# A hybrid decoder trunk: where the product with VO of the last chunk and M and VO of the first heads stand in the order of work

## The chip, the core and the metric

The program runs on one core of one Trainium2 chip. The metric is device time in microseconds (us) of one execution, lower is better. The core has TensorE (PE, matmuls), VectorE (DVE), ScalarE (ACT), GpSimd (POOL) and SyncE (SP), each with a queue of its own, and DMA engines; they meet only at semaphores.

## The reference

One layer, 2048 prompt tokens and 8 samples, width 1024, all in fp32. The part that the change touches:

```
h = rmsnorm(x, g_cross); q = (h @ wq_c) in 4 heads of 256
s = q @ mem_k.T / 16 ; a = softmax(s) ; o = a @ mem_v          # mem_k = mem @ wk_c, mem_v = mem @ wv_c, 256 memory tokens
x = x + o @ wo_c
h = rmsnorm(x, g_ffn); up = h @ w_up ; c = causal depthwise conv of width 3 (up)
x = x + (silu(c_gate) * c_act) @ w_down
```

Ahead of it stand an input projection of rmsnorm(x) @ w_in to pooling channels, q, k and v, a pooling mixer, a differential attention and an output projection; behind it a last rmsnorm.

## The kernel before, in words

**Tiles.** The prompt is cut into four chunks of 512 tokens (c = 0 to 3; the samples ride with chunk 3). Activations lie transposed, 128 channels on the partitions. Each fp32 operand is split in two: `hi`, a cast on ACT, and `lo`, the rest, a subtraction on DVE (`split`, L94 and L95; for weights `whi` L307 and `wlo` L310, for half weights `whl` L327 and L329). A product is three matmuls (L99 to L101): hi by lo, hi by hi, lo by hi.

**Memory side.** For each head two matrices are made once. M = wq_c(head) mem_k.T (`m_head`: 16 transposes `wqT` L540, then 48 matmuls of 256 columns) gives the scores from h in one product; VO = mem_v wo_c(head) (`vo_head`, 24 matmuls of 512 columns) gives the output from the softmax in one. Both go to DRAM and come back as weights later. `p0_items((0, 1))` makes those of heads 0 and 1 at the start of the program; its list is cut into `kv0`, `m0`, `kv1`, `m1`: keys and values of head 0, M and VO of head 0, and the same for head 1. `half` is the list of input projections `z` (L483) of chunks 0 and 1, with the pooling products `pool` among them; `n1[c]` the norm of chunk c that they need.

**Cross-attention of a chunk** (`p3_items`): `sc_` has per head the scores S in PSUM (96 matmuls of 256 columns), then the softmax: maximum on DVE (`mx`, L1274), `nbx`, four exponentials on ACT (E, L1280), reciprocal and scaling on DVE (L1281, L1282). E is transposed by PE (AT, L1302) and split into Ahi and Alo; the transposes are put off by a delay counted in cost, and forced when the next part needs them. `vo` begins with a reload of x, then has 8 tiles of 24 matmuls of 512 columns, each followed by an add to x on DVE (L1327), and a store. S takes one of two large PSUM buffers, which the up products take too.

**Feed-forward** (`ffn_items`): 22 pairs of an activation tile and a gate tile, in groups of 4, 4, 4, 4, 4 and 2. A pair is seven products of 12 matmuls of 256 columns (L1613, L1615), an algorithm with fewer multiplications, whose sums of inputs (`xop_items`: `t`, `x` L1573, and their splits `xhi`, `xlo`) and of weights (`sums_items`: stored as `s_d`, loaded as `shl`) are made beforehand; the adds of its results are DVE's `s` and `Uf` (L1618). The `down` products (L1729) of a group run among the pairs of the next. `n3` is the norm ahead of it (h3sq L228, scales L271).

**What sets the order.** All work of the program is one list of items, put together by hand at the end of the kernel, and run from front to back by `drive`; every engine takes its instructions in the order in which they are then issued. An item has a cost `i[2]` and a latency `i[3]`. `weave(main, extra, lo, hi)` spreads the list `extra` over the list `main`: from the share lo of main's cost to the share hi. `look(a, b, c)` sets how many weights ahead of their use the load (SP), the cast (ACT) and the subtraction (DVE) are issued.

Of the kernel before, what the change touches and what calls it, by code (L numbers as in the profile page):

```python
# [48 lines left out]
def tile_trunk_step(ctx: ExitStack, tc: tile.TileContext, a, o):  # L49
# [306 lines left out]
    def item(specs, fn, cost=0.0, lat=0.0):  # L356


        return (specs, fn, cost, max(lat, cost, 0.3))
# [17 lines left out]
    def weave(main, extra, lo=0.0, hi=1.0):  # L377

        tm, te = sum(i[2] for i in main) or 1.0, sum(i[3] for i in extra) or 1.0
        out, k, dm, de = [], 0, 0.0, 0.0  # L380
        for i in main:
            out.append(i)
            dm += i[2]
            while k < len(extra) and lo + (hi - lo) * (de / te) <= dm / tm:
                out.append(extra[k])
                de += extra[k][3]
                k += 1
        return out + extra[k:]
# [978 lines left out]
    def both(key, name, src, write):  # L1367

        def fn(n):
            def run(ws):  # L1370
                ps = PB("sx")
                for kt in range(KT):
                    for z in range(2):
                        PE.matmul(ps[:2 * NS, :256], src[:, kt].rearrange("p z b -> p (z b)"), ws[kt // 4][z][:, kt % 4, :],
                                  start=kt == 0 and z == 0, stop=kt == KT - 1 and z == 1)
                if n == 0:
                    sx[key] = H("sx")
                S.copy(sx[key][:2 * NS, n * 256:(n + 1) * 256], ps[:2 * NS, :256])
                if n == 3:
                    later(2.0, write)  # L1380
            return run
        return [item([cols256(name, n * 256, 0), cols256(name, n * 256, 1)], fn(n), 2.0) for n in range(4)]
# [110 lines left out]
    sc_items = both("q", "wq_c", h2st, sc_qwrite) + [item([], lambda _: None, 0, 5.0)]  # L1493
# [272 lines left out]
    def tail_half(t):  # L1766
        def fn(_):
            ps, m = tail_turn(t, 0)
            V.tensor_tensor(tail["y"][t][:m, :512], ps[:m, :512], tail["g"][:m, :512], ALU.mult)
        return item([], fn, 0.5)  # L1770
# [69 lines left out]
                         t[:FT, :512].rearrange("n (b p) -> n b p", b=4))  # L1840


    def ffn_items(c, xops):


        out, dn, j = [], dn0.pop() if dn0 else [], 0
        for g in GROUPS:
            if j == GROUPS[0]:
                out.append(item([], ffn_open(c)))
            last = j + g == NF  # L1850
            for i in range(g):
                u = ffn_up(c, j + i)
                k = (2, 1)[i] if last else (2, 3, 3, 0)[i]
                d, dn = dn[:k], dn[k:]
                at = (5, 6, 7) if i == 0 else (2, 4, 6)
                for k, up in enumerate(u):
                    out.append(up)
                    if last and i == g - 1:
                        out += xops[k - 1:k] if k else []
                    if k + 1 in at:  # L1860
                        out += d[:1]
                        d = d[1:]
            if last:
                out += xops[6:]
            out += dn
            dn = ffn_down(c, j, g)
            j += g
        if c == NCH - 1:
            return out + [item([], conv_out)] + dn[:5] + [tail_half(t) for t in range(3)] + dn[5:7] + [
                tail_half(t) for t in range(3, 5)] + dn[7:] + [item([], tail_out)]  # L1870
        dn0.append(dn)
        return out

    dn0 = []
    n1 = [norm1_items(c) for c in range(NCH)]
# [3 lines left out]
    def raw_open(_):  # L1879
# [5 lines left out]
    half = p1_items((0, 1))  # L1885
    pre = p0_items((0, 1))
    att01, att23 = att_items((0, 1)), att_items((2, 3))
    kv0, m0, kv1, m1 = pre[1:13], pre[13:23], pre[23:35], pre[35:]
    order = pre[:1] + [item([], vec_load), look(4, 3, 2)] + kv0[:6] + n1[0][0] + kv0[6:] + [item([], vec_turn)]
    order += weave(weave(kv1, m0), n1[0][1][:3] + n1[1][0] + n1[0][1][3:], 0.1, 1.0)  # L1890
    order += weave(weave(half[:12], m1), [item([], pool_load), item([], lambda_)] + n1[1][1], 0.2, 1.0)
    order += [look(3, 2, 1)]
    order += weave(weave(half[12:24] + [item([], pool_prep)] + half[24:-8], sums_items(range(5)), 0.0, 0.6),
                   n1[2][0] + n1[2][1] + n1[3][0] + n1[3][1][:5] + [item([], att_table)], 0.65, 1.0)
    order += att01[0] + weave(half[-8:], n1[3][1][5:])
    late = p1_items((2, 3))
# [3 lines left out]
    wo, n2, sc_, vo, n3 = zip(*p3)  # L1900
# [3 lines left out]
    order += weave(vo[0], n2[1], 0.0, 0.9)  # L1904
    order += weave(sc_[1] + wo[2], sample_items, 0.0, 0.95)
    order += weave(vo[1] + sc_[2][:8], merge(n2[2], sample_items2[:-2]) + sample_items2[-2:], 0.0, 0.55)
    order += weave(sc_[2][8:] + wo[3] + weave(vo[2], n2[3], 0.0, 0.9) + weave(sc_[3] + vo[3], n3[0] + xop_items(0), 0.4, 1.0),
                   sums_items(range(16, NF)), 0.0, 0.85)
    xops = [xop_items(c) for c in range(1, NCH)] + [[]]
    order += [look(6, 3, 2)]  # L1910
    order += weave(ffn_items(0, xops[0]), sc_items + n3[1], 0.02, 0.9)
    order += weave(ffn_items(1, xops[1]), final(0) + sc_items2 + n3[2], 0.2, 0.9)
    order += weave(ffn_items(2, xops[2]), final(1) + n3[3], 0.2, 0.9)
    order += weave(ffn_items(3, xops[3]), final(2), 0.2, 0.5)
# [30 lines left out]
```

## Time and profile before

| | |
|---|---|
| median of 3 runs | 3116.74 us (3115.84 to 3120.43) |
| the profiled execution | 3116.27 us, its span 3114.6 us |
| mean granted clock of PE | 0.978 |
| PE, DVE, ACT, POOL busy | 94%, 72%, 43%, 17% |

The times of the rows are in us from the start of the span. A hole in front of an instruction is given in brackets with what ended it. In the program, the input projections of the first two chunks begin at 67 us; the scores of the last chunk end at about 1558 us, its product with VO runs until 1615 us, and the first group of four pairs until about 1690 us.

### The profile page before, as it was taken

How to read it: one execution, taken by the hardware profiler on the slowest of the kernel's cores; microseconds unless marked ns; L12 is line 12 of the kernel's file. 1: busy time of each engine (PE TensorE's matmuls, PEld its weight loads, DVE VectorE, ACT ScalarE, POOL GpSimd, SP SyncE). 2: the span in 40 equal slices, each digit the busy share in tenths (PEclk: the TensorE clock that was granted, in tenths of full speed). 3: DMA queues.
4: the chain of work that ended last, by engine and by line, in shares of the span. 5: the costliest groups of instructions: out<-in, count | busy, mean ns of one | idle time of the engine just before them, and what ended most of it. 6: DMA issues, size and time to landing. Idle time of an engine off the chain costs nothing.

```text
span 3114.6 us, 52466 instructions
## 1 busy us (share of the span) xinstructions
PE 2939.9 (94%) x19806; PEld 2650.3 (85%) x19806; DVE 2240.0 (72%) x4032; ACT 1351.9 (43%) x2271; POOL 516.2 (17%) x961
## 2 busy tenths in 40 slices
PE   7999899889899898999989999999999999999998
PEld 6778789778788687689978899888899989999998
DVE  5734666467776668666778978888888777877777
ACT  5534445355665442334333344444444433443333
POOL 0244235312111115421000000010000010000000
PEclk9999999989999999999999999999999999999999
DMA  8777478835353357658759876687776786576762
GB/s 280 243 270 241 135 238 263 265 97 186 115 173 119 110 176 255 203 171 282 276 190 332 294 247 220 211 275 249 238 253 217 236 291 209 178 262 218 240 210 105
DMA packets 520511, 683.14 MB, mean 219 GB/s; under 512 B 27472, under 2 KB 342359, under 8 KB 520243
## 3 DMA queue, kind: packets, MB, share of 16 engines
q1 hardware_dynamic: 466525, 533.87, 52.8%
q0 software_dynamic: 39936, 135.17, 12.2%
q10 hardware_dynamic: 13798, 10.76, 1.1%
q8 instruction: 156, 2.56, 0.3%
q14 instruction: 96, 0.79, 0.1%
HBM read 549.12 MB, written 130.98 MB: 218 GB/s over the span
## 4 chain that ended last, share of the span: by engine, by line
PE 59%; DVE 8%; issue 4%; DMA 2%; ACT 2%; POOL 1%; DVEq 0%; ACTq 0%; POOLq 0%; SPq 0%
PE up L1613 15%; PE down L1729 15%; PE up L1615 7%; PE wo L483 3%; PE upB L1613 2%; PE S L99 2%; PE S L101 2%; PE S L100 2%; PE O L1163 2%; PE vo L99 1%; PE vo L100 1%; PE vo L101 1%; PE upB L1615 1%; PE sc L1111 1%; DVE T L1122 1%
## 5 line engine op out<-in xcount | busy, mean ns | idle before, releaser
L1729 PE MATMUL down<-act,whi 128*128 128x512 f32 (+1 forms) x1760 | 452.1, 351 | 3.2 <-ACT whi L307 3.1
L1613 PE MATMUL up<-xhi,shl 128*128 128x256 f32 (+1 forms) x2816 | 406.9, 285 | 7.9 <-DVE s L1618 6.3
L1613 PEld LDWEIGHTS up<-xhi,shl 128*128 128x128 f32 x2816 | 365.1, 188 | 37.9 <-DVE s L1618 13.2
L1667 ACT ACTIVATE cc<-Uf,vec 128x512 f32<-128x512 f32 (+1 forms) x176 | 143.9, 818 | 502.6 <-DVE Uf L1618 491.6
L310 DVE TENSOR_TENSOR wlo<-wraw,whi 128x1024 fp32r<-128x1024 f32 x256 | 310.2, 1220 | 38.5 <-ACT whi L307 30.2
L1729 PEld LDWEIGHTS down<-act,whi 128*128 128x128 f32 x1760 | 286.5, 189 | 36.6 <-ACT whi L307 3.5
L307 ACT CAST whi<-wraw 128x1024 fp32r<-128x1024 f32 x256 | 265.3, 1047 | 102.3 <-DMA wraw<-in_w_down_dram 29.3
L1729 PE MATMUL down<-act,wlo 128*128 128x512 f32 (+1 forms) x880 | 280.2, 350 | 0.1
L1672 POOL COPY halo<-Uf 128x2 f32<-128x2 f32 x176 | 56.7, 322 | 1275.5 <-DVE Uf L1618 1250.5
L1129 ACT ACTIVATE T<-T,mn 128x1024 f32<-128x1024 f32 (+4 forms) x192 | 171.9, 897 | 131.2 <-DVE mn L1122 120.5
L1615 PE MATMUL up<-xlo,shl 128*128 128x256 f32 (+1 forms) x1408 | 223.8, 281 | 0.0
L1111 PE MATMUL sc<-K,Q 128*128 128x512 f32 (+5 forms) x640 | 176.6, 394 | 37.8 <-DVE mn L1122 36.3
L1613 PE MATMUL up<-xhi,whl 128*128 128x256 f32 (+1 forms) x1408 | 199.3, 284 | 8.8 <-DVE whl L329 4.9
L1613 PEld LDWEIGHTS up<-xhi,whl 128*128 128x128 f32 x1408 | 183.9, 189 | 17.5 <-DVE whl L329 6.1
L1615 PEld LDWEIGHTS up<-xlo,shl 128*128 128x128 f32 x1408 | 191.3, 188 | 0.3
L1675 DVE SCALAR_TENSOR_TENSOR cc<-Uf,vec,cc 128x512 f32<-128x512 f32 x176 | 131.6, 748 | 73.6 <-ACT cc L1667 73.5
L329 DVE TENSOR_TENSOR whl<-wraw,whl 128x512 fp32r<-128x512 f32 x264 | 178.5, 683 | 0.4 <-ACT whl L327 0.4
L1733 DVE TENSOR_TENSOR xf<-xf,down 128x512 f32<-128x512 f32 (+1 forms) x240 | 134.9, 578 | 56.2 <-PE down L1729 55.0
L1729 PEld LDWEIGHTS down<-act,wlo 128*128 128x128 f32 x880 | 154.1, 188 | 22.5 <-DVE wlo L310 0.9
L1122 DVE CUSTOM_DVE_ANT_0 T<-sc,Dt 128x1024 f32<-128x1024 f32 (+7 forms) x128 | 125.8, 985 | 64.0 <-PE sc L1111 49.3
L1618 DVE TENSOR_TENSOR Uf<-up,s 128x256 f32<-128x256 f32 (+1 forms) x264 | 111.6, 423 | 83.0 <-PE up L1615 80.5
L327 ACT CAST whl<-wraw 128x512 fp32r<-128x512 f32 x264 | 155.2, 614 | 25.4 <-PE up L1615 6.4
(437 smaller groups left out, 7124.5 us busy)
## 6 DMA issues: line engine op xcount, KB each, us to landing
shl<-s_d SPq DMA_DIRECT2D x352, 512.0 KB
wraw<-in_w_up_dram SPq DMA_DIRECT2D x264, 256.0 KB
wraw<-in_w_down_dram SPq DMA_DIRECT2D x88, 512.0 KB
s_d<-shi POOLq DMA_DIRECT2D x44, 512.0 KB
s_d<-slo POOLq DMA_DIRECT2D x44, 512.0 KB
wraw<-in_w_in_dram SPq DMA_DIRECT2D x32, 512.0 KB
Q<-q_d SPq DMA_DIRECT2D x64, 256.0 KB
wraw<-in_w_out_dram SPq DMA_DIRECT2D x32, 512.0 KB
```

The source lines that it names most:

```text
L307: S.copy(self.hi[:, :1024], self.raw[:, :1024])
L310: V.tensor_tensor(self.lo[:, :1024], self.raw[:, :1024], f(self.hi[:, :1024]), ALU.subtract)
L327: S.copy(self.hl[:, :512], self.raw)
L329: V.tensor_tensor(self.hl[:, 512:1024], self.raw, f(self.hl[:, :512]), ALU.subtract)
L1111: PE.matmul(ps[:, j * 512:j * 512 + w], v3(Q[c], 2)[:, z, self.t * P:(self.t + 1) * P], K[c][hf][:, c0:c0 + w], start=z == 0, stop=z == 1)
L1122: V.tensor_tensor_reduce(out, pin, din, -SLOPE[self.h], 3.0e38 if hf == 0 else mn[:, 0:1], ALU.add, ALU.min, mn[:, hf:hf + 1])
L1129: S.activation(tg[:, :mg], tg[:, :mg], AF.Exp, bias=mn[:, last:last + 1], scale=-1.0, accum_out=self.l[:, 2 * g + c:2 * g + c + 1])
L1613: PE.matmul(out, wi[:, k, :], xh[:, k], start=k == 0 and wi is wl, stop=False)
L1615: PE.matmul(out, wh[:, k, :], xl[:, k], start=False, stop=k == 3)
L1667: S.activation(cc[:, :w], U[:, 2:2 + w], AF.Identity, bias=vc(CB + nt), scale=vc(CWT + 2 * FT + nt))
L1729: PE.matmul(out, st["w"][0][wi][:, p, n0:n0 + P], act[:, z + c0:z + c0 + n], start=st_ and p == 0, stop=en and p == g - 1)
L1733: V.tensor_tensor(xx[:, c0:c0 + n], xx[:, c0:c0 + n], out, ALU.add)
```

## The change

It changes only the order of the list; each engine has the same instructions as before. (1) `ffn_items` takes a list `begin`, spread over the first group's up products from 25% to 95%; for chunk 0 it is the last chunk's product with VO without its first item, the reload of x. The samples' work and the norm of chunk 1 then begin at 15% of that part instead of 2%. (2) In the stretch ahead, the main list is the last chunk's scores alone, and the norm of chunk 0, its operands and that reload are spread over it from 5%; before it was the scores and the product, and they were spread from 40%. (3) At the start, `kv1` stands with the norms alone; `m0` goes among the first 12 items of `half`, where `m1` was; `m1` goes among the rest of `half`, from 10% to 40%.

```diff
@@ -1840,7 +1840,7 @@
                          t[:FT, :512].rearrange("n (b p) -> n b p", b=4))
 
 
-    def ffn_items(c, xops):
+    def ffn_items(c, xops, begin=None):
 
 
         out, dn, j = [], dn0.pop() if dn0 else [], 0
@@ -1862,6 +1862,8 @@
                         d = d[1:]
             if last:
                 out += xops[6:]
+            if begin and j == 0:
+                out = weave(out, begin, 0.25, 0.95)
             out += dn
             dn = ffn_down(c, j, g)
             j += g
@@ -1887,10 +1889,10 @@
     att01, att23 = att_items((0, 1)), att_items((2, 3))
     kv0, m0, kv1, m1 = pre[1:13], pre[13:23], pre[23:35], pre[35:]
     order = pre[:1] + [item([], vec_load), look(4, 3, 2)] + kv0[:6] + n1[0][0] + kv0[6:] + [item([], vec_turn)]
-    order += weave(weave(kv1, m0), n1[0][1][:3] + n1[1][0] + n1[0][1][3:], 0.1, 1.0)
-    order += weave(weave(half[:12], m1), [item([], pool_load), item([], lambda_)] + n1[1][1], 0.2, 1.0)
+    order += weave(kv1, n1[0][1][:3] + n1[1][0] + n1[0][1][3:], 0.1, 1.0)
+    order += weave(weave(half[:12], m0), [item([], pool_load), item([], lambda_)] + n1[1][1], 0.2, 1.0)
     order += [look(3, 2, 1)]
-    order += weave(weave(half[12:24] + [item([], pool_prep)] + half[24:-8], sums_items(range(5)), 0.0, 0.6),
+    order += weave(weave(weave(half[12:24] + [item([], pool_prep)] + half[24:-8], m1, 0.1, 0.4), sums_items(range(5)), 0.0, 0.6),
                    n1[2][0] + n1[2][1] + n1[3][0] + n1[3][1][:5] + [item([], att_table)], 0.65, 1.0)
     order += att01[0] + weave(half[-8:], n1[3][1][5:])
     late = p1_items((2, 3))
@@ -1904,11 +1906,11 @@
     order += weave(vo[0], n2[1], 0.0, 0.9)
     order += weave(sc_[1] + wo[2], sample_items, 0.0, 0.95)
     order += weave(vo[1] + sc_[2][:8], merge(n2[2], sample_items2[:-2]) + sample_items2[-2:], 0.0, 0.55)
-    order += weave(sc_[2][8:] + wo[3] + weave(vo[2], n2[3], 0.0, 0.9) + weave(sc_[3] + vo[3], n3[0] + xop_items(0), 0.4, 1.0),
+    order += weave(sc_[2][8:] + wo[3] + weave(vo[2], n2[3], 0.0, 0.9) + weave(sc_[3], n3[0] + xop_items(0) + vo[3][:1], 0.05, 1.0),
                    sums_items(range(16, NF)), 0.0, 0.85)
     xops = [xop_items(c) for c in range(1, NCH)] + [[]]
     order += [look(6, 3, 2)]
-    order += weave(ffn_items(0, xops[0]), sc_items + n3[1], 0.02, 0.9)
+    order += weave(ffn_items(0, xops[0], vo[3][1:]), sc_items + n3[1], 0.15, 0.9)
     order += weave(ffn_items(1, xops[1]), final(0) + sc_items2 + n3[2], 0.2, 0.9)
     order += weave(ffn_items(2, xops[2]), final(1) + n3[3], 0.2, 0.9)
     order += weave(ffn_items(3, xops[3]), final(2), 0.2, 0.5)
```

The first piece of the order is PE at the start, where the input projections z of chunk 0 begin. Before:

```order
L483 MATMUL z<-h1hi,wlo 128x512
L483 MATMUL z<-h1hi,whi 128x512
L483 MATMUL z<-h1lo,whi 128x512 x8
L540 MATMUL wqT<-ident,wraw 128x128 x12
L99 MATMUL M<-mkvT,wqhi 128x256
```

After, at the same place, and further on, among the z of the pooling channels (`phi` and `plo` are the split input of the pooling product):

```order
L483 MATMUL z<-h1hi,wlo 128x512
L483 MATMUL z<-h1hi,whi 128x512
L483 MATMUL z<-h1lo,whi 128x512 x8
L540 MATMUL wqT<-ident,wraw 128x128 x12
L99 MATMUL M<-mkvT,wqhi 128x256
```

```order
L483 MATMUL z<-h1lo,whi 128x512 x2
L540 MATMUL wqT<-ident,wraw 128x128 x8
L483 MATMUL z<-h1lo,whi 128x512 x6
L99 MATMUL pool<-plo,pws 128x512
L100 MATMUL pool<-phi,pws 128x512
L101 MATMUL pool<-phi,pws 128x512
L835 MATMUL psum<-spl 128x8 x4
```

The 16 transposes in front of an M stand at the first place in both; before they are head 1's, after head 0's. Head 1's are moved behind, to the second place, ahead of the pooling product.

The second piece is DVE in the scores of the last chunk, up to the reduce of the last head (the last L1274). Before, from the reduce of the third head (first row) on:

```order
L1274 TENSOR_REDUCE mx<-S 128x4
L1275 TENSOR_SCALAR nbx<-mx 128x4
L310 TENSOR_TENSOR wlo<-wraw,whi 128x1024
L1281 RECIPROCAL rcx<-lx 128x4
L310 TENSOR_TENSOR wlo<-wraw,whi 128x1024
L1282 TENSOR_TENSOR E<-E,rcx 128x1024
L1531 TENSOR_TENSOR wg<-wg 128x512
L1532 TENSOR_TENSOR wg<-wa,wg 128x512
L1528 TENSOR_TENSOR wa<-wg,wa 128x512
L1529 TENSOR_TENSOR wa<-wa 128x512
L1274 TENSOR_REDUCE mx<-S 128x4
L1275 TENSOR_SCALAR nbx<-mx 128x4
```

After, the same end of the stretch, from the seventh row behind the reduce of the third head:

```order
L95 TENSOR_TENSOR xlo<-x_14765,xhi 128x2x256
L1573 TENSOR_TENSOR x_14763<-x_14765,x_14763 128x2x256
L329 TENSOR_TENSOR whl<-wraw_15069,whl 128x512
L1281 RECIPROCAL rcx<-lx 128x4
L95 TENSOR_TENSOR xlo<-x_14762,xhi 128x2x256
L1282 TENSOR_TENSOR E<-E,rcx 128x1024
L95 TENSOR_TENSOR xlo<-x_14763,xhi 128x2x256
L95 TENSOR_TENSOR xlo<-x_14764,xhi 128x2x256
L95 TENSOR_TENSOR xlo<-x_14765,xhi 128x2x256
L1573 TENSOR_TENSOR x_14764<-x_14764,t_15116 128x2x256
L1573 TENSOR_TENSOR x_14765<-x_14765,t_15116 128x2x256
L1274 TENSOR_REDUCE mx<-S 128x4
```

Between two reduces there now stand the sums and splits of chunk 0's operands, and the first half weight `whl` of the feed-forward.

The third piece is PE at the end of the scores. Before:

```order
L100 MATMUL S<-whi,h2hi 128x256
L101 MATMUL S<-whi,h2lo 128x256
L1302 MATMUL AT<-ident,E 128x128 x16
L99 MATMUL vo<-Alo,whi 128x512
L100 MATMUL vo<-Ahi,whi 128x512
L101 MATMUL vo<-Ahi,wlo 128x512
```

After, at the end of the scores, and then from the fifth product of the first pair on:

```order
L100 MATMUL S<-whi,h2hi 128x256
L101 MATMUL S<-whi,h2lo 128x256
L1613 MATMUL up<-xhi,whl 128x256 x8
L1615 MATMUL up<-xlo,whl 128x256 x4
L1613 MATMUL up<-xhi,shl 128x256 x8
L1615 MATMUL up<-xlo,shl 128x256 x4
L1613 MATMUL up<-xhi,shl 128x256 x8
```

```order
L1613 MATMUL upB<-xhi,whl 128x256 x8
L1615 MATMUL upB<-xlo,whl 128x256 x4
L1613 MATMUL up<-xhi,shl 128x256 x8
L1615 MATMUL up<-xlo,shl 128x256 x4
L1302 MATMUL AT<-ident,E 128x128 x16
L1613 MATMUL up<-xhi,whl 128x256 x8
L1615 MATMUL up<-xlo,whl 128x256 x4
L99 MATMUL vo<-Alo,whi 128x512
L100 MATMUL vo<-Ahi,whi 128x512
L101 MATMUL vo<-Ahi,wlo 128x512
```

The first product of the first pair follows the scores directly, the transposes of the heads 2 and 3 come six products later, and the product with VO begins behind the seventh, in small pieces among the up products.

## Rows read from the trace of the kernel before

**Rows 1.** The page, busy time of the engines, and the chain that ended last.

```profile
PE 2939.9 (94%) x19806; PEld 2650.3 (85%) x19806; DVE 2240.0 (72%) x4032; ACT 1351.9 (43%) x2271; POOL 516.2 (17%) x961
...
PE 59%; DVE 8%; issue 4%; DMA 2%; ACT 2%; POOL 1%; DVEq 0%; ACTq 0%; POOLq 0%; SPq 0%
```

**Rows 2.** Windows: from:to length, busy PE PEld DVE ACT POOL, PEclk, DMA share, GB/s.

```profile
1560.00:1570.00 10.00, 3.65 (x13) 3.23 (x14) 9.49 (x13) 4.52 (x12) 0.00 (x0) 0.66 0.33 105
1570.00:1620.00 50.00, 50.00 (x242) 41.41 (x241) 38.60 (x64) 18.12 (x27) 4.37 (x9) 1.00 0.57 193
1620.00:1690.00 70.00, 62.01 (x451) 54.70 (x452) 49.12 (x80) 31.45 (x49) 4.46 (x20) 0.95 0.88 311
1680.00:1690.00 10.00, 6.79 (x20) 4.82 (x19) 8.71 (x11) 4.35 (x6) 0.00 (x0) 0.66 1.06 392
```

**Rows 3.** Timeline of PE: start, us, what, idle before and its releaser.

```profile
1557.41 0.28 PE L100 MATMUL S<-whi,h2hi 128*128 128x256 f32 x1
1557.53 0.28 PE L101 MATMUL S<-whi,h2lo 128*128 128x256 f32 x1
1557.65 1.04 PE L1302 MATMUL AT<-ident,E 128*128 128x128 f32 x8
1566.35 1.94 PE L1302 MATMUL AT<-ident,E 128*128 128x128 f32 x8 [7.67 <-DVE E L1282]
1567.99 0.80 PE L99 MATMUL vo<-Alo,whi 128*128 128x512 f32 x1
...
1569.44 0.51 PE L99 MATMUL vo<-Alo,whi 128*128 128x512 f32 x1
...
1683.43 2.07 PE L1729 MATMUL down<-act,whi 128*128 128x512 f32 x4 [3.07 <-ACT whi L307]
```

**Rows 4.** Timeline of DVE, last scores to first group.

```profile
1521.97 1.22 DVE L1274 TENSOR_REDUCE mx<-S 128x4 f32<-128x1024 f32 x1 [7.25 <-PE S L101]
...
1557.85 1.23 DVE L1274 TENSOR_REDUCE mx<-S 128x4 f32<-128x1024 f32 x1 [2.69 <-PE S L101]
...
1559.18 3.88 DVE L228 TENSOR_TENSOR h3sq<-h3sq 128x1024 f32<-128x1024 f32 x3
...
1564.78 0.17 DVE L1281 RECIPROCAL rcx<-lx 128x4 f32<-128x4 f32 x1
1564.98 1.22 DVE L1282 TENSOR_TENSOR E<-E,rcx 128x1024 f32<-128x1024 f32 x1
...
1584.95 2.74 DVE L271 SCALAR_TENSOR_TENSOR x<-x,vec,R 128x512 f32<-128x512 f32 x4 [1.94 <-ACT R L260]
...
1590.86 1.28 DVE L95 TENSOR_TENSOR xlo<-x,xhi 128x512 fp32r<-128x512 f32 x2
...
1618.51 0.42 DVE L1618 TENSOR_TENSOR s<-up,s 128x256 f32<-128x256 f32 x1 [2.96 <-PE up L1615]
```

**Rows 5.** Timeline of ACT, its last read of the last scores.

```profile
1561.09 0.21 ACT L1280 ACTIVATION_READ_ACCUMULATOR E<-S,nbx 128x1 f32 x1
```

**Rows 6.** Waits, 1500 to 1700: us in total, times, longest.

```profile
PE up L1613 <- DVE s L1618: 2.7, 4, 1.2
```

**Rows 7.** Timeline of PE at the start: VO of head 0, transposes of head 1.

```profile
56.91 0.39 PE L99 MATMUL VO<-wlo,mkvT 128*128 128x512 f32 x1
57.14 0.40 PE L100 MATMUL VO<-whi,mkvT 128*128 128x512 f32 x1
...
75.12 1.09 PE L540 MATMUL wqT<-ident,wraw 128*128 128x128 f32 x8 [0.64 <-DMA wraw<-in_wq_c_dram]
80.69 1.12 PE L540 MATMUL wqT<-ident,wraw 128*128 128x128 f32 x4 [4.48 <-DVE wqlo L95]
```

**Rows 8.** DMA view of 10 to 90 us: packets and mean rate.

```profile
DMA packets 18248, 20.63 MB, mean 258 GB/s; under 512 B 1329, under 2 KB 15435, under 8 KB 18243
```

**Rows 9.** Timeline of PE, pool products that waited.

```profile
151.43 0.51 PE L99 MATMUL pool<-plo,pws 128*128 128x512 f32 x1 [1.95 <-DVE plo L95]
...
159.61 0.50 PE L99 MATMUL pool<-plo,pws 128*128 128x512 f32 x1 [1.62 <-DVE plo L95]
```

## The prediction

> **What bounds the kernel now.** I read the page first: TensorE (PE) is busy 94% of the span and holds 59% of the chain that ended last, VectorE (DVE) is busy 72% and holds 8% of that chain [rows 1]. So a change in the order of work can only win where PE stands still, and the reader should look for those places, not at the totals. Next the windows by stage [rows 2]: PE is full in 1570:1620, which is the product with VO of the last chunk, and has holes just before it (3.65 of 10 us busy in 1560:1570) and behind it (62.01 of 70 in 1620:1690, the first group of four pairs of the feed-forward). Third, PE's own rows at those holes [rows 3]: 7.67 us of idle time before the transposes of the last scores, released by the normalised exponentials E that DVE writes, and 3.07 at 1683.43, the longest hole in the first group. Fourth, DVE's rows in that place [rows 4], because it is the engine waited for.
>
> Losses of PE in this place, as they stand: the 7.67; the half clock behind it; 70 - 62.01 = 7.99 of holes in the group; the half clock behind the 3.07. The half clock is taken from rows: eight transposes took 1.94 behind the hole and 1.04 before it (0.9 lost), three VO products took 1569.44 - 1567.99 = 1.45 where three at 0.23 [rows 7] need 0.70 (0.75 lost), together 1.65, say 1.7. The granted clock is 0.66 in 1680:1690 too [rows 2], so I take 1.7 there as well. Sum 7.67 + 1.7 + 7.99 + 1.7 = 19.1 us.
>
> A rule on the same thing: the Trainium skill, "TensorE: Matmul & The Clock Gate", section Terms, prices a throttle at the throttled time times one minus the granted share. A mean of 0.66 over 10 us is 6.8 us at the lower of the two levels, 3.4 lost for each place. By that rule the sum below would come to -4.9 instead of -3.2 in this place. The rows contradict it here, because part of those 6.8 us PE was idle anyway, so 1.7 is used.
>
> **Part one: the score stretch of the last chunk.** Nothing is added or removed, only moved. Before, the norm of chunk 0 and the splits of its operands (xhi, xlo, and their differences t) were spread from 40% of scores plus product to the end; now they lie beside the scores alone, from 5% on. The second piece of the order shows what that does between the reduces of two heads on DVE. I add up the DVE rows of the changed order with durations of [rows 4]: a reduce 1.22, a 128x1024 subtraction, E among them, 1.22, h3sq 3.88 for three, a scale of the norm 2.74 / 4 = 0.68 (the same for every 128x512 subtraction or add), an xlo or t half 0.64, a small one 0.17.
> - Reduce of head 0 to that of head 1: one reduce, four 0.69, h3sq 3.88 + 0.68, three 1.22 and six small: 13.2 us.
> - Head 1 to head 2: one reduce, ten small, two splits of the sums 2.44, eight scales 5.47, E 1.22, two weight splits 2.44, four halves 2.56: 16.9 us.
> - Head 2 to head 3: one reduce, fourteen halves 8.96, two Alo 1.28, whl 0.68, E 1.22 and the small ones: 15.0 us with rounding.
>
> That is 45.1 us of work, where before the reduces of head 0 and 3 stand 1557.85 - 1521.97 = 35.9 apart, each waiting for PE. So DVE, not PE, now sets the pace there: from 1521.97 the reduces come at 1535.2, 1552.1 and 1567.1. Before its eight scales DVE once more waits for the row sums spread by PE and copied by ACT; that wait was 1.94 at 1584.95 and I put 1.9 there, so 1554.0 and 1569.0.
>
> PE ends its scores at 1557.85 and some tenths for the norm's small products, say 1558.2. Its next work is now not the transposes but the first product of the feed-forward (third piece of the order), which needs whl; whl stands 9.75 us behind the reduce of head 2 (that reduce, ten halves, Alo among them as 0.64 each, with nbx and whl itself), at 1563.75. **Wait 5.5.** Two products of 12 matmuls at 0.12 [rows 3] and one hand-over between them of 0.7 (2.7 in four [rows 6]) end at 1567.3. The third product needs PE's bank that DVE empties by the add into s, and that add stands behind the reduce of head 3: 1569.0 + 1.22 + two halves 1.28 + 0.17 + 0.42 = 1572.1. **Wait 4.8.** One more hand-over 0.7. The transposes of heads 2 and 3 stand behind six products and find E ready. So the 7.67 does not vanish, it becomes 5.5 + 4.8 + 1.4 = 11.7. Half clock behind the first wait is swallowed by the second, behind the second it costs 1.7.
> Bounds: without the 1.9 it is 9.8; with 3.0 more, if ACT hands over E as late as DVE's rows before show at worst (an estimate from 1.94 and half as much again), 14.7.
>
> **Part two: the first group.** The product, 192 matmuls at 0.23, 45 us of PE work that depends on nothing in the group, now lies among the up products from 25% to 95%. DVE was busy 49.1 of 70 us there [rows 2]; with eight adds of 0.68 and eight weight splits of 1.22 it has 64 of 115. Each hole between a product and the add that frees its bank now has 1.4 us or more of VO products in it. I let the short holes go; of the 3.07 with its 1.7, which hangs on ACT's cast of a weight for the down product at the end of the group, where little of the product is left, I keep half: 2.5. Bounds 0 and 9.7 (all stays).
> Sum of both parts: 11.7 + 1.7 + 2.5 = 15.9 against 19.1, **-3.2**; from 9.8 (-9.3) to 14.7 + 3.4 + 9.7 = 27.8 (+8.7). The sums for the feed-forward's weights, which are spread over the stretch ahead, come 45 us of main work denser; PE is full in that stretch or waits for others, so I cost that at nothing; without the cover it is inside the bounds.
>
> **Part three: the start.** M and VO of head 0 leave the stretch before the first input projection z: 48 products at 0.12, 24 at 0.23 and 16 transposes at 1.09 / 8 [rows 3, 7], 13.5 us of PE. All of it comes back among the z products, as head 1's. What is won is how much earlier z starts. At most 13.5; at least what the DMAs give, as four loads of 0.52 MB leave the queue of SP ahead of the input weights, at 258 GB/s [rows 8] 8.1 us. I take the middle, 10.8. The first piece of the order shows head 0 standing among z just where head 1 stood, so the 4.48 that the transposes wait for wqlo [rows 7] should stay. But the later work of head 1 stands ahead of pool products that waited 1.95 and 1.62 for plo from a full DVE [rows 9]; 13.5 us more PE work for some 5 us more of DVE work covers that 3.6. Term: 13.5 - 10.8 - 3.6 = **-0.9**; from +5.4 (8.1, nothing covered) to -8.1 (13.5, and the 4.48 gone too).
>
> **Sum.** -3.2 - 0.9 = -4.1 from the profiled execution's 3116.27 (span 3114.6 and 1.67 around it): 3112.2. That execution lies 0.47 below the median of the runs shown, so on their scale 3112.6.
>
> **The rivals.**
> - *DVE's delay is carried on* (slower). The 9 us by which the reduce of head 3 is late are not worked off in the first pairs, as each up product there needs an add and a split weight from the same queue in order; the product with VO waits for Alo behind them as well. Then all of the group's 9.7 stays, the wait at the head of it is 14.7 and both clock losses 3.4 count: +8.7, with the start +7.8, 3124.5. It decides from the point where the first up product starts over 8.5 us behind the scores. For it: before, the reciprocal at 1564.78 ran at once when the row ahead ended, 3.4 us after its last input on ACT [rows 4, 5], so three h3sq on DVE already cost PE that much. Against: 64 of 115 us. The Trainium skill, same page, section on the array's architecture, says that VectorE takes its queue strictly first in, first out; the reciprocal's row agrees, and by that rule alone this rival would be the forecast if nothing gave DVE time to recover.
> - *Covered fully* (faster). In the place of the feed-forward all but the 9.8 goes: -9.3, with the start -10.2, 3106.5. Or the start also loses its 4.48, with -3.2: 3108.1. For both: VO's products need nothing new, and DMA in the group asks less per us. Against: the rows of head 0 among z are the same as head 1's were.
> - *It only trades places* (no change). z starts only 8.1 earlier, the pool covers (+1.8), and the whole 3.07 + 1.7 stays: 11.7 + 1.7 + 4.8 = 18.2 (-0.9): +0.9, 3117.6.
>
> **How the numbers follow.** What a measurement of this kernel can tell from no change is about 0.2%, 6.2 us: faster below 3110.5, slower above 3123.0. Forecast 0.38, and its own range 3108 to 3117 gives 0.14 faster and 0.24 no change. Covered fully 0.27, all faster. Trades places 0.16, no change but for 0.03. Carried on 0.19, of which 0.17 slower. That is 0.41 faster, 0.39 no change, 0.20 slower. The range for 8 in 10 goes from 3101, past both covered cases, to 3124, just short of the whole of the carried one.
>
> **What would show it.** In the changed profile: no hole of 7 us before the transposes of heads 2 and 3; instead PE waiting 4 to 7 us for whl at its first up product and 3 to 6 for s at the third; DVE above 9 of 10 from the reduce of head 1 on, with the last reduce 8 to 12 us behind its scores; the first group above 97% of PE; the first z 9 to 13 us earlier, the hole before M about 4.5 as before, no wait for plo behind M of head 1. I am wrong if the reduces are on time, if the holes in the group stay, or if the time is won ahead of 300 us.

## The result, and the profile after

The changed kernel takes **3135.51 us** (median of 5 runs, 3134.87 to 3137.59); the kernel before took 3119.0 beside it (3115.84 to 3125.17). The ratio is 1.0053, 95% interval [1.0039, 1.0068]: slower by some 16.5 us, where 4.1 us faster was forecast, and outside the range. The profiled execution of the changed kernel has a span of 3133.2 us at a mean clock of 0.974 [rows 1 for before]. The page, busy time and chain:

```profile
PE 2950.1 (94%) x19806; PEld 2660.7 (85%) x19806; DVE 2239.9 (71%) x4032; ACT 1356.8 (43%) x2271; POOL 526.7 (17%) x961
...
PE 58%; DVE 9%; issue 4%; DMA 2%; ACT 2%; POOL 1%; DVEq 0%; ACTq 0%; POOLq 0%; SPq 0%
```

The same 19806 matmuls take 10 us more of busy PE. Since both kernels issue the same instructions, I compared the start times of the same ones:

| PE instruction | before | after | after minus before |
|---|---|---|---|
| first z | 67.06 | 56.79 | -10.27 |
| 200th z | 145.36 | 149.86 | +4.50 |
| first score product of the first attention | 298.53 | 314.55 | +16.02 |
| first AT of the last head of chunk 2 | 1415.60 | 1433.28 | +17.68 |
| first S of the last chunk | 1510.39 | 1530.28 | +19.89 |
| first down product | 1683.43 | 1697.78 | +14.35 |
| 300th down product | 1878.66 | 1895.59 | +16.93 |

Nearly all of the loss is made before 300 us (at the 200th z part of head 1's products is still to come, so the +4.50 there is not yet all that was lost). The place of the feed-forward gains 5.5 us between its scores and the first down product, and gives most of that back on either side: 2.2 ahead of the scores and 2.6 behind the first down product.

**The start.** Windows up to the first score product (from:to length, busy PE PEld DVE ACT POOL, PEclk, DMA share, GB/s), and three stretches of 20 us in it. Before:

```profile
0.00:298.53 298.53, 272.66 (x1587) 235.90 (x1588) 165.57 (x266) 142.16 (x227) 85.59 (x182) 0.97 0.78 259
40.00:60.00 20.00, 17.53 (x121) 15.95 (x120) 12.20 (x35) 10.27 (x22) 2.84 (x4) 0.83 0.67 227
60.00:80.00 20.00, 15.07 (x82) 11.41 (x80) 15.78 (x22) 13.38 (x22) 2.00 (x13) 0.95 0.92 286
100.00:120.00 20.00, 19.06 (x83) 15.12 (x82) 17.38 (x27) 9.96 (x15) 2.75 (x7) 1.00 0.81 249
```

After:

```profile
0.00:314.55 314.55, 280.27 (x1587) 242.77 (x1588) 164.30 (x264) 141.22 (x226) 86.97 (x182) 0.95 0.75 247
40.00:60.00 20.00, 15.57 (x94) 14.05 (x95) 15.02 (x43) 11.28 (x24) 2.85 (x4) 0.76 0.75 250
60.00:80.00 20.00, 14.94 (x70) 12.55 (x69) 13.29 (x22) 11.94 (x23) 2.63 (x14) 0.76 0.54 175
100.00:120.00 20.00, 16.45 (x60) 12.86 (x59) 16.28 (x25) 9.41 (x13) 5.40 (x9) 0.83 0.45 143
```

Both windows hold 1587 matmuls. PE's idle time goes from 298.53 - 272.66 = 25.9 to 34.3 us (+8.4), and the busy time of the same matmuls from 272.66 to 280.27 (+7.6): the granted clock fell from 0.97 to 0.95 on the mean, to 0.76 in 40:80. PE's rows after, those that waited (answering to [rows 7, 9]):

```profile
41.48 0.47 PE L623 MATMUL R<-ident,ry 128*128 128x128 f32 x1 [4.66 <-DVE ry L193]
...
56.79 0.80 PE L483 MATMUL z<-h1hi,wlo 128*128 128x512 f32 x1 [1.85 <-ACT h1hi L637]
...
72.12 0.69 PE L540 MATMUL wqT<-ident,wraw 128*128 128x128 f32 x2 [4.49 <-DVE wqlo L95]
...
104.58 0.79 PE L99 MATMUL pool<-plo,pws 128*128 128x512 f32 x1 [3.55 <-DVE plo L95]
...
147.45 0.47 PE L99 MATMUL pool<-plo,pws 128*128 128x512 f32 x1 [1.74 <-DVE plo L95]
...
160.74 0.79 PE L99 MATMUL pool<-plo,pws 128*128 128x512 f32 x1 [5.36 <-DVE plo L95]
```

The hole before M is 4.49 as it was 4.48. The waits for plo are 10.65 in all, against 0.94 + 1.95 + 1.62 = 4.5 before. R waits 4.66 where it waited 2.33, and z now waits for the norm, 1.85: without M and VO of head 0 there, PE has nothing to do while DVE and ACT make the norm. Behind the two long waits for plo PE runs at the lower of its two clock levels, granted 0.50:

```profile
160.74:163.00 2.26, 2.26 (x5) 1.81 (x6) 1.68 (x2) 0.58 (x1) 1.25 (x3) 0.50 0.99 329
```

The pool product takes 0.79 there, against 0.50 before [rows 9]; behind the wait of 1.74 it took 0.47. How the longest wait for plo arises is seen in DVE's rows after, from the sums Wn of the pooling chain to plo:

```profile
152.40 0.70 DVE L692 TENSOR_TENSOR Wn<-Wn 128x521 f32<-128x521 f32 x1
153.01 0.69 DVE L1529 TENSOR_TENSOR wa<-wa 128x512 f32<-128x512 f32 x1
155.38 0.69 DVE L692 TENSOR_TENSOR Wn<-Wn 128x513 f32<-128x513 f32 x1 [1.68 <-DMA m_d<-ms]
155.99 1.22 DVE L310 TENSOR_TENSOR wlo<-wraw,whi 128x1024 fp32r<-128x1024 f32 x1
157.12 0.69 DVE L696 SCALAR_TENSOR_TENSOR pr<-Wn,U 128x512 f32<-128x512 f32 x1
157.73 1.22 DVE L310 TENSOR_TENSOR wlo<-wraw,whi 128x1024 fp32r<-128x1024 f32 x1
158.86 1.22 DVE L95 TENSOR_TENSOR slo<-wg,shi 128x1024 fp32r<-128x1024 f32 x1
160.00 0.69 DVE L95 TENSOR_TENSOR plo<-pr,phi 128x512 fp32r<-128x512 f32 x1
```

The chain Wn, pr, plo is interleaved with two weight splits and a sum's split, 3.66 us, and stalls 1.68 more; the profile puts that stall down to the store of M. In the kernel's text the tiles of this chain (U, Wn, pr, phi, plo, pm) and the copies `ms` of M and `vos` of VO take turns in one ring of six staging buffers (`St`), so a copy of M that waits for its store can hold up a Wn. PE thus waits for a short chain that stands in a long queue, and in part, it seems, for a buffer.

The first of the three waits, 3.55 at 104.58, is not of this kind. Head 1's first transposes come only at 126.2, and on DVE the chain stands there among the scales and splits (`h1lo`) of chunk 1's norm:

```profile
99.31 0.68 DVE L696 SCALAR_TENSOR_TENSOR pr<-Wn,U 128x512 f32<-128x512 f32 x1
...
102.70 1.22 DVE L281 TENSOR_TENSOR h1lo<-xT,h1hi 128x1024 fp32r<-128x1024 f32 x1
103.84 0.69 DVE L95 TENSOR_TENSOR plo<-pr,phi 128x512 fp32r<-128x512 f32 x1
```

How head 1's place in the list makes this one longer (0.94 before) is not shown.

**The place of the feed-forward.** DVE's reduces of the last scores after [rows 4 for before]:

```profile
1543.18 1.22 DVE L1274 TENSOR_REDUCE mx<-S 128x4 f32<-128x1024 f32 x1 [6.39 <-PE S L101]
...
1555.77 1.22 DVE L1274 TENSOR_REDUCE mx<-S 128x4 f32<-128x1024 f32 x1
...
1573.52 1.22 DVE L1274 TENSOR_REDUCE mx<-S 128x4 f32<-128x1024 f32 x1
...
1587.35 1.23 DVE L1274 TENSOR_REDUCE mx<-S 128x4 f32<-128x1024 f32 x1
```

They stand 12.6, 17.8 and 13.8 us apart (forecast 13.2, 18.8 and 15.0), and only the first still waits for PE. PE after the scores [rows 3 for before]:

```profile
1580.14 0.28 PE L101 MATMUL S<-whi,h2lo 128*128 128x256 f32 x1
1582.78 1.18 PE L1613 MATMUL up<-xhi,whl 128*128 128x256 f32 x8 [2.36 <-DVE rcx L1281]
...
1584.89 1.21 PE L1613 MATMUL up<-xhi,shl 128*128 128x256 f32 x8 [0.46 <-ACT s L1628]
...
1590.24 2.08 PE L1613 MATMUL up<-xhi,shl 128*128 128x256 f32 x8 [3.67 <-DVE s L1618]
...
1593.68 2.08 PE L1613 MATMUL up<-xhi,shl 128*128 128x256 f32 x8 [0.52 <-DVE s L1618]
...
1599.17 2.04 PE L1613 MATMUL upB<-xhi,whl 128*128 128x256 f32 x8 [2.56 <-DVE whl L329]
```

Windows of the same stretch and of what follows, after [rows 2 for before]:

```profile
1580.00:1590.00 10.00, 3.75 (x28) 3.16 (x26) 10.00 (x18) 6.41 (x18) 0.00 (x0) 0.93 0.61 209
1590.00:1600.00 10.00, 6.69 (x28) 6.13 (x29) 4.74 (x9) 3.90 (x11) 0.21 (x2) 0.50 1.00 392
1600.00:1700.00 100.00, 100.00 (x632) 87.43 (x632) 62.93 (x95) 42.16 (x61) 5.81 (x22) 0.99 0.76 257
```

The hole before the transposes is gone, five waits (9.6 us) took its place, and behind them the first group has no holes at all (100.00 of 100 us). Behind the group new waits appear in PE's rows, for weights that DVE splits too late:

```profile
1736.74 0.50 PE L1729 MATMUL down<-act,wlo 128*128 128x512 f32 x1 [1.06 <-DVE wlo L310]
...
1755.77 2.03 PE L1613 MATMUL up<-xhi,whl 128*128 128x256 f32 x15 [1.76 <-DVE whl L329]
```

The windows from the first to the 300th down product, before and then after: PE's idle time goes from 2.0 to 5.2 us.

```profile
1683.43:1878.66 195.23, 193.19 (x1299) 176.35 (x1300) 170.53 (x273) 78.33 (x123) 7.95 (x48) 0.99 0.84 280
1697.78:1895.59 197.81, 192.61 (x1314) 176.09 (x1313) 172.91 (x275) 78.53 (x122) 10.52 (x50) 1.00 0.83 284
```

### The profile page after: what moved, and what is told of

Read it like the earlier page. It is cut to its first block, busy times and chain, and to the rows that moved or that the text cites. A ratio compares the mean times of both kernels' runs of the same rounds, so it can differ in the third digit from the quotient of the medians.

```text
span 3133.2 us, 52517 instructions
## 1 busy us (share of the span) xinstructions
PE 2950.1 (94%) x19806; PEld 2660.7 (85%) x19806; DVE 2239.9 (71%) x4032; ACT 1356.8 (43%) x2271; POOL 526.7 (17%) x961
## 4 chain that ended last, share of the span: by engine, by line
PE 58%; DVE 9%; issue 4%; DMA 2%; ACT 2%; POOL 1%; DVEq 0%; ACTq 0%; POOLq 0%; SPq 0%
PE up L1613 15%; PE down L1729 14%; PE up L1615 7%; PE wo L483 3%; PE upB L1613 2%; PE O L1163 2%; PE S L99 1%; PE vo L99 1%; PE vo L100 1%; PE S L100 1%; PE vo L101 1%; PE S L101 1%; PE sc L1111 1%; PE upB L1615 1%; DVE T L1122 1%
## 5 line engine op out<-in xcount | busy, mean ns | idle before, releaser
L483 PE MATMUL z<-h1hi,wlo 128*128 128x512 f32 (+1 forms) x480 | 162.2, 370 | 8.2 <-DVE pps L708 5.3
```

What stands on the lines that cost most here:

```text
L483: PE.matmul(out, w[wi][:, kt, :], kslice(z, kt, c0, n), start=i == 0, stop=i == 3 * KT - 1)
```

## The experiments

Theories for the start: A1, what is lost is head 0's M and VO as cover beside the norms; A2, it is head 1's M and VO beside the pooling products; A3, the loads and splits look too short ahead; D, a form of A2, DVE's queue with the sums in it makes plo late. For the place of the feed-forward: B, DVE's queue there sets the time, ahead of the group and behind it. Ratios are to the kernel before, timed beside, with 95% intervals.

**One half of the change at a time.** The changed start with the feed-forward of before, and the reverse; the edits are the three lines of the start, and the others, of the diff above.

> Only the edit of the start (kv1 alone, m0 among the first input projections, m1 among the later ones); all else as before. Theory A (the start itself loses: 15.7 us by the first key transposes at 202 us of before, half idle time, half half clock, and none of it comes back): 3131 to 3137 us, and the first key transposes 15 to 16.5 us later than before. Rival (the late start only shifts work that would have waited anyway, and the loss is made by the two parts together): under 3125 us.

Measured: 3136.55 us, 1.0038 [1.0022, 1.0055]. The time is as expected; the first key transposes come 13.5 us later than before, not 15 or more.

> Start as before; the norm of chunk 0 for the feed-forward beside the last scores and the product with VO among the first pairs, as in the change. From the two traces: +2 us in 200 to 1415 and +2 in 1415 to 1510 (denser sums), +2.7 in the scores, -8.3 from the end of the scores to the first down product, +4.4 behind it: +1 to +4 us, 3119 to 3122. Rival (the parts behind the start only lose because they run with the shifted start): -4 to -8, 3110 to 3114.

Measured: 3120.37 us, 0.9995 [0.998, 1.001]. So the start makes the loss, and the new place makes no difference that can be measured; its gain up to the first down product and 5.0 us of idle time behind it are both in its trace.

**Which move of the start.** Head 0 as before, head 1 late:

```diff
-    order += weave(weave(half[:12], m1), [item([], pool_load), ...
+    order += weave(half[:12], [item([], pool_load), ...
-    order += weave(weave(half[12:24] + ... + half[24:-8], sums_items(range(5)), 0.0, 0.6),
+    order += weave(weave(weave(half[12:24] + ... + half[24:-8], m1, 0.1, 0.4), sums_items(range(5)), 0.0, 0.6),
```

> M and VO of head 0 stay beside the keys and values of head 1, as before; only m1 moves, from the first input projections to the later ones (10% to 40%), as in the change. Theory A1 (the loss comes from taking m0 away from the stretch ahead of the input projections, whose waits it filled): 3114 to 3122 us, first key transposes within 4 us of before. Theory A2 (the loss comes from m1 beside the pooling chain, whose casts and splits queue on ACT and DVE): 3127 to 3135, and waits of PE for plo above 8 us.

Measured: 3128.54 us, 1.0022 [1.0005, 1.004]. Head 1's place alone slows it; plo waits 6.5 in all, less than the 8 that A2 had. Up to the first score product that is 3.5 us, of the 8.3 by which the medians differ. In its trace 3.8 us more come between the last S and the first down product, where the list is the same as before; why is not shown.

The changed start, with head 1 later still:

```diff
-    order += weave(weave(weave(half[12:24] + ... + half[24:-8], m1, 0.1, 0.4), ...
+    order += weave(weave(weave(half[12:24] + ... + half[24:-8], m1, 0.5, 0.9), ...
```

> The edit of the start, but m1 spread from 50% to 90% of the later input projections, behind the pooling products, where PE is full and DVE is busy 4 of 20 us in the kernel before. Theory A1 (m0 taken from the stretch ahead): still 8 us or more slower, 3127 to 3135. Theory A2 (m1 beside the pooling chain): 3116 to 3122, waits of PE for plo back at 4 to 5 us.

Measured: 3121.31 us, 1.0003 [0.9984, 1.0021]. Its windows row up to the first score product, and the one wait for plo left over 0.9 us:

```profile
0.00:302.36 302.36, 275.27 (x1586) 238.60 (x1587) 162.78 (x264) 139.57 (x225) 85.61 (x180) 0.96 0.78 257
```

```profile
102.44 0.50 PE L99 MATMUL pool<-plo,pws 128*128 128x512 f32 x1 [0.94 <-DVE plo L95]
```

The early waits are still there (R 4.65, z 1.87, M 4.49), and the time is that of the kernel before. A1 falls as the whole cause: with head 1 late, head 0's move costs nothing that the timing can tell from none. A2 holds, with a limit: head 1's place between 10% and 40% costs 16.3 us by the medians when head 0 has moved too, and 8.3 when it hasn't, and the intervals of the two overlap. In the traces, up to the first score product, head 1's move alone costs 3.5 us, head 0's with head 1 late 3.8, and both of the change together (the start alone) 13.8. So in these single traces the two moves make each other worse; no run shows how.

**Why that place.** Deeper look-ahead from the end of the norms on:

```diff
     order += weave(kv1, n1[0][1][:3] + n1[1][0] + n1[0][1][3:], 0.1, 1.0)
+    order += [look(6, 5, 4)]
```

> The edit of the start, and only the look-ahead of its second stretch raised from 4, 3, 2 weights to 6, 5, 4, so that the two raw weights of M of head 1, which stand in the list ahead of the next input weights, don't keep these from being loaded, cast and split early. Theory A3 (m1 does harm because its weights fill the look-ahead and push the input weights' casts and splits into the stretch where DVE is already full): waits for plo 4 to 6 us in all instead of 10.2 in the edit of the start alone, first key transposes 3 to 8 us later than before, time 3 to 8 us over before. Theory A2 (m1's own casts and splits on ACT and DVE do it, however early the input weights come): waits for plo stay at 9 to 11, +12 to +16.

Measured: 3142.35 us, 1.0071 [1.0047, 1.0095]. Worse, 21 us over before, more than either theory gave: plo still waits 2.90, 1.38 and 4.39, and a z waits 3.11 for ACT's copy of VO. A3 falls.

The pooling products put off twice as far:

```diff
-    later(6.0, mix)
+    later(12.0, mix)
```

> The edit of the start, with the pooling products put off by 12 instead of 6 units of cost behind their z, so that PE reaches them after DVE has made plo. What PE waits for is taken away, the work on DVE stays. If the waits for plo and the half clock behind them are the loss: -10 us of waits and -4 of clock against the edit of the start alone, first key transposes within 3 us of before, time -2 to +4 us against before. If DVE is the bound of the stretch, another wait takes their place (for z's inputs or weights) and the time stays 10 or more above before.

Measured: 3132.65 us, 1.0043 [1.0028, 1.0059]. All waits for plo are gone, but others (2.00, 1.12 and 1.29, for ACT's pm and ms) take their place. The first score product is 3.9 us earlier than in the run of the changed start alone, and the timed ratio is not better: the waits for plo by themselves are not the loss. DVE's longest wait in that chain is now, as the profile names it, for a store of M, which would be the ring of staging buffers:

```profile
153.40 0.71 DVE L692 TENSOR_TENSOR Wn<-U 128x527 f32<-128x527 f32 x1 [6.68 <-DMA m_d<-ms]
```

The sums taken from beside head 1:

```diff
-    ... half[24:-8], m1, 0.1, 0.4), sums_items(range(5)), 0.0, 0.6),
+    ... half[24:-8], m1, 0.1, 0.4), sums_items(range(5)), 0.4, 0.8),
```

> The changed start alone, with one more edit: the sums of the first five feed-forward weights (per weight pair four adds of 0.69 us and two splits of 1.22 us on DVE, and their loads, casts and stores) spread from 40% to 80% of the later projections instead of from the start to 60%, so that M and VO of head 1 (10% to 40%) have them no longer beside them. Theory D (M and VO of head 1 cost there because DVE takes their splits, the sums and the pooling chain strictly in order, so that plo comes late): the waits of PE for plo, 10.2 us in the run of the changed start alone, fall below 4, the first key product comes 5 us or more earlier than in that run (there 13.5 later than in the kernel before), and the time is within 6 us of the kernel before. Rival (the hand-overs between PE, ACT and DVE inside M and VO themselves, and the earlier waits for the norm, cost it, and the sums have nothing to do with it): waits and first key product within 2 us of that run, 3131 to 3138 us. A second rival (the sums are only late somewhere else): plo waits fall, but the same time is lost before 300 us or in the attention behind.

Measured: 3134.91 us, 1.0045 [1.0031, 1.006]. PE's rows with the waits that count, and the windows row:

```profile
102.93 0.79 PE L99 MATMUL pool<-plo,pws 128*128 128x512 f32 x1 [3.55 <-DVE plo L95]
...
152.83 0.50 PE L99 MATMUL pool<-plo,pws 128*128 128x512 f32 x1 [0.95 <-DVE plo L95]
...
207.73 0.50 PE L483 MATMUL z<-h1hi,wlo 128*128 128x512 f32 x1 [1.35 <-DVE ql L728]
...
212.99 0.33 PE L748 MATMUL kT<-ident,kf 128*128 128x128 f32 x1 [2.19 <-ACT kf L738]
```

```profile
0.00:313.73 313.73, 278.00 (x1586) 238.77 (x1587) 165.92 (x264) 139.90 (x225) 85.06 (x181) 0.97 0.74 247
```

The waits for plo fall from 10.2 to 4.5, not quite below D's 4, and the 400th z comes 6.7 us earlier than with the changed start alone; but the first key transposes come only 2.7 us earlier (D: 5 or more), by the first score product all of it is lost again, behind ql and kf, where the sums now stand, and the time is 15 us over before. The second rival holds: the sums only choose where the time is lost. D falls.

The start in one table, up to the first score product, with the same work in front of it in each (from the windows rows):

| kernel | us | PE idle | PE busy | ratio |
|---|---|---|---|---|
| before | 298.5 | 25.9 | 272.7 | 1 |
| changed | 314.6 | 34.3 | 280.3 | 1.0053 |
| start alone | 312.4 | 35.6 | 276.8 | 1.0038 |
| head 0 as before | 302.1 | 29.6 | 272.5 | 1.0022 |
| head 1 late | 302.4 | 27.1 | 275.3 | 1.0003 |
| pooling put off | 308.5 | 30.0 | 278.5 | 1.0043 |
| sums later | 313.7 | 35.7 | 278.0 | 1.0045 |

**The place of the feed-forward.** All of these but the last have the start of before and the changed feed-forward, with one edit or two. The samples' work and the norm of chunk 1 from 2% again:

```diff
-    ... sc_items + n3[1], 0.15, 0.9)
+    ... sc_items + n3[1], 0.02, 0.9)
```

> Start as before, the place of the change, but the samples' work and the norm of chunk 1 begin at 2% of the first feed-forward, as before, and not at 15%. Theory B (behind the first group the change loses 3 to 4 us since DVE, put off by 13%, is full for 100 us there): the holes of PE from the first down product to the 300th shrink from some 5 to 2 us, time 2 to 4 us below that of the place alone. Rival (that DVE work then stands in the first group and makes the ups wait): the gain from the end of the scores to the first down product, 7 to 8 us, shrinks by the same 3.

Measured: 3116.49 us, 0.9983 [0.9972, 0.9995]. PE's idle time between the first and the 300th down product is 0.8 us, against 5.0 without the edit. The median is 3.9 us below that of the place alone, as B had it, but the intervals of the two ratios overlap.

The norm of chunk 0 spread from the product with VO of chunk 2 on:

```diff
-    ... + weave(vo[2], n2[3], 0.0, 0.9) + weave(sc_[3], n3[0] + xop_items(0) + vo[3][:1], 0.05, 1.0),
+    ... + weave(weave(vo[2], n2[3], 0.0, 0.9) + sc_[3], n3[0] + xop_items(0) + vo[3][:1], 0.25, 1.0),
```

> Start as before, the place of the change, but the norm of chunk 0 and its operands are spread from 25% of the product with VO of chunk 2 and the last scores together, not over the last scores alone. If DVE's 45 us between the first and the last reduce (36 available) are what makes PE wait at the first up products: the last reduce comes at most 3 us behind the end of its scores (7.4 in the change), the waits at the first pair fall from 9.6 to under 4 us, time 5 to 8 us below that of the place alone. Rival: the work is as much in the way beside the product with VO, PE waits there or tiles run out, and the time stays within 3 us.

Measured: 3118.88 us, 0.999 [0.9977, 1.0003], not told apart from before, and 1.5 us below the place alone where 5 to 8 were expected. The waits at the first pair fall as forecast, to 2.2, and from the last S to the first down product it takes 106.3 us instead of 118.6, but the scores begin later and the waits behind the group stay (5.0). Both edits together:

> Start as before; the place of the feed-forward as changed, with two more edits together: the samples' work from 2% again, and the norm and operands of chunk 0 spread from 25% of the product with VO of chunk 2 and the last scores. Theory B (DVE's queue ahead of and behind the first group sets this place, so that work moved off it in both directions is won twice): stretch from the end of the last scores to the first down product about 108 to 112 us (before 126.2), the next 195 us without more than 2 us of waits, 3108 to 3114 us, faster than before and than each edit alone (3116.5 and 3118.9). Rival (the norm moved ahead only costs the stretch ahead of the scores, as its start came 18 us later in the run with that edit alone): 3117 to 3121.

Measured: **3110.65 us, 0.9973 [0.9961, 0.9984]**, the fastest of all, 8 to 9 us below the kernel before. Its window from just before the end of the scores to just before the first down product, and PE's longest wait in it:

```profile
1570.00:1680.00 110.00, 107.25 (x694) 93.32 (x694) 81.06 (x117) 47.58 (x81) 7.65 (x22) 1.00 0.88 302
```

```profile
1580.51 0.74 PE L1613 MATMUL up<-xhi,shl 128*128 128x256 f32 x4 [1.07 <-DVE s L1618]
```

The granted clock stays at 1.00, and from the last S to the first down product it takes 108.5 us (before 125.9). Most of that is work moved ahead, as the scores begin 12.3 us later than before: in the traces the first down product comes 2.2 us earlier, the 300th 4.8. Its interval overlaps that of the samples' edit alone, so that the second edit adds to the first is likely and not shown. The same with the norm from 50% instead of 25%:

> As the run with both edits and the start of before, but the norm of chunk 0 spread from 50% instead of 25%, so only over the last scores and little ahead. Theory B: between the run with the samples' edit alone and the run with both, 3111 to 3117 us. Rival (the earlier norm is what costs): faster than the run with both by 2 us or more.

Measured: 3113.77 us, 0.9983 [0.9971, 0.9994]. PE has a wait of 5.50 again behind the scores:

```profile
1574.34 1.01 PE L1613 MATMUL up<-xhi,whl 128*128 128x256 f32 x3 [5.50 <-ACT E L1280]
```

It lies where B has it, between the samples' edit alone and both, but the intervals overlap. Last, both edits with the changed start and head 1 from 50% to 90%:

> As the run with both edits in the place of the feed-forward, and the changed start with M and VO of head 1 spread from 50% to 90% of the later projections. Theory A2 (the loss of the start is M and VO of head 1 beside the pooling products): first key product of the attention's start as in the run of that start alone, no wait for plo over 1 us, and the time within 3 us of the run with both edits and the start of before. Rival (taking head 0's M and VO from beside the norms costs by itself, PE idle ahead of z): 5 or more us slower than that run.

Measured: 3112.94 us, 0.9977 [0.9968, 0.9986], 2.3 us from the run with the start of before. The changed start with head 1 late shows neither gain nor loss.

## Why the prediction was wrong

**Part three is the step that failed.** It forecast -0.9 for the start; the mark at the first score product shows +16.0. Its working began well: the first z is 10.27 us earlier (10.8 forecast), and the hole before M stayed at 4.5. That the first came so near is in part luck: 10.8 was the middle between a bound of PE work and one of the loads, and what held z back in the end was the norm, with waits of 4.66 at R and 1.85 at z that neither bound knew. The failing sentence is that 13.5 us more PE work for some 5 us more of DVE work "covers that 3.6". Instead of shrinking by 3.6 (or staying), the waits for plo went from 4.5 to 10.65. I had weighed total work on the two engines; the rows above point to where in DVE's queue a short chain stands, and head 1's splits, copies and stores entered that chain's stretch at the longest wait, which grew from 1.62 to 5.36. (The first grew from 0.94 to 3.55 ahead of head 1's transposes, the middle one not at all.) The runs show head 1's place to be what the loss hangs on: with head 1 behind the pooling products the timed loss is gone, with the start else as changed. Why that place costs so much is argued, not shown. Two more errors lie in the same term, and the second is as large. Earlier work that stood beside the norms was cover for PE: R went from 2.33 to 4.66, and z waits 1.85. And I counted idle time only: the 7.6 us of busy time that came with the lower clock were nowhere in the term, though I had priced half clock at each hole of the feed-forward. The Trainium skill, "TensorE: Matmul & The Clock Gate", section Terms, prices a throttle at throttled time times one minus the granted share; by the two windows an estimate by it is 314.55 x 0.05 less 298.53 x 0.03, 6.8 us, and the rows' 7.6 agrees within the rounding of the clock.

**Part one was right in mechanism.** DVE set the pace, its work between reduces came out within 1.2 us of the sums, and no hole of 7 us stood before the transposes. The waits at the head of the group were 9.6, forecast 11.7 (bounds 9.8 to 14.7): the one for whl was 2.36 instead of 5.5 (the releaser named, rcx, stands right behind whl), since the scores themselves took longer, 49.9 us from the first S to the last instead of 47.1. In them S waited 1.1 for a split weight, and ahead of them R of a norm waited 1.3, both of which are not in the kernel before; I take them for the cost of the sums 45 us denser, which I had put at nothing.

**Part two was right and short.** The first group has 100.00 of 100 us (2.5 of holes forecast). But the text never priced the third edit there, the samples' work put off from 2% to 15%. It took work out of the group, where DVE is now only 62.93 of 100 us busy, into the stretch behind, and the way to the 300th down product grew by 2.6 us, with 3.2 us more idle time. Taking that one number back gave 0.9983, and the idle time there fell to 0.8. From that AT of chunk 2 to the 300th down product the place is -0.75 instead of -3.2, which agrees with its own timing, 0.9995 [0.998, 1.001].

**The rivals.** *DVE's delay is carried on* had the right sign for the wrong place: its own mark, a first up product over 8.5 us behind the scores, came at 2.4, and the delay was worked off in the first group. *Covered fully* asked for 9.3 us in this place or no hole before M; neither came. *It only trades places* describes the feed-forward. That the start could cost more than 5.4 us stood nowhere: its bounds came from when z begins, and a loss behind z had no rival. None of the three signs of being wrong was this one: ahead of 300 us I watched for time won, not for time lost. Only the mark "no wait for plo behind M of head 1" failed where the loss is.

**What stays open.** That the loss of the changed start hangs on head 1's place is shown; which of its instructions make it, and why it came out twice as large with head 0's move, is not. Neither deeper look-ahead, nor later pooling products, nor later sums brought the time back: each only moved the waits. That DVE's queue carries the delay is read from the rows above, not shown by a run. A rival stands untested: the ring of six staging buffers that head 1's copies share with the pooling chain. Stores of M held up a Wn for 1.68 us in the changed kernel and for 6.68 with the pooling products put off; a run with a larger ring, or a ring of their own for the copies, would tell.

## What to carry to other kernels

Work moved off the front of a program is not won by how much earlier the next stage begins: look at what PE waits for in the stage that receives it, and whether a short dependent chain shares a queue there with the work that comes along. Price the clock with each hole. Every small number of such an edit deserves its own term: one of them (15% for 2%) left 5.0 us of idle time where 0.8 was possible. The best version came with DVE's work moved out of the crowded stretch, both ahead and behind; every run with this place changed keeps the product with VO in the first group, so what that move is worth by itself is not shown.

## What the hardware showed that I had not expected

Waiting cost about twice itself at the start: 8.4 us more idle time came with 7.6 us more busy time for the same 1587 matmuls. It is no fixed factor: with head 0 as before, 3.7 us more idle time came with no more busy time, and the granted clock was 0.98.

```profile
0.00:302.05 302.05, 272.50 (x1586) 235.02 (x1587) 163.40 (x263) 138.72 (x224) 84.88 (x180) 0.98 0.78 257
```

And executions of one and the same kernel spread from 3112 to 3133 us, so that single traces of this kernel place a loss, but only the medians size it.
